# g0's rows turned by TensorE between idle matmuls, and the norm weights of the last row multiplied ahead of its norm

## The chip, the cores and the metric

The kernel runs on one core of one Trainium2 chip. A core has five engines that work side by side: TensorE (PE in the profile, its weight loads PEld), VectorE (DVE), ScalarE (ACT), GpSimd (POOL) and SyncE (SP). Each takes its own instructions in order; they wait for each other through semaphores. SyncE issues most transfers, ScalarE and GpSimd issue some; all of them run on the same 16 DMA engines. The metric is the time of one execution on the device, in microseconds (us), lower is better; the time before is the median of 3 runs.

## What is computed

A trunk of two layers over two independent sequences, a prompt of 2048 tokens and a sample of 512, with 1024 channels, all in float32:

```python
def trunk(x, ...):
    x = attention_layer(x, attn_norm[0], ...)     # layer 0
    x = fourier_layer(x, fourier_norm[0], ...)    # layer 1
    return rmsnorm(x, final_norm)

def rmsnorm(x, g):
    inv = lax.rsqrt(jnp.mean(x * x, axis=-1, keepdims=True) + 1e-6)
    return x * inv * g

def attention_layer(x, g, w_in, w_out, sink, rel_bias):
    z = rmsnorm(x, g) @ w_in                      # q, k, v and a gate
    o = banded_gqa_with_sink(q, k, v, rel_bias, sink)
    return x + (o * jax.nn.silu(gate)) @ w_out

def fourier_layer(x, g, w_gate, w_out):
    h = rmsnorm(x, g)
    f = jnp.fft.fftn(h.reshape(b, s, 4, 256), axes=(1, 3), norm="ortho").real
    return x + (f * jax.nn.silu(h @ w_gate)) @ w_out
```

`attn_norm[0]` is called g0 in the kernel, `final_norm` gf. The change touches how g0 reaches the chip's memory and how the last 128 rows of the result get their final norm.

## The kernel before

Tokens are worked on in tiles of 128 rows (the partitions of the on-chip memory). The attention phase takes five chunks of 512 tokens; chunk 0 is the sample. The Fourier phase follows and writes the outputs, a few tiles of 128 rows at a time.

Every float32 product is made of three: an operand is split into a coarse part (hi, a cast on ScalarE) and the rest (lo, a difference on VectorE or GpSimd), and `matmul3` (L92 to L95) adds hi*hi, hi*lo and lo*hi in one accumulator. So an operand takes two steps on two engines before its three matmuls can run, and all these matmuls stand under line 95 in the profile. A tile framework with its own scheduler places the instructions on each engine and sets the semaphores; `after(a, b)` only asks that a be issued behind b.

**The start.** At L61 to L63 the kernel makes small constants and asks, from ScalarE's queue, for g0 as a tile `g0s` of 128 partitions and 8 columns: partition p holds g0[k*128 + p] in column k. Twelve matmuls of zeros (`WARM`, L239 to L242) keep TensorE at work until the first operands are there; their zeros come from a VectorE memset. Meanwhile the first projection weight (k, 512 KB) comes in two halves, one from SyncE's queue and one from ScalarE's (`half`, L249 to L255), and is split into `wk`. `make_h` (L202) loads the transposed input in eight slices `xk` of 128 channels and 512 tokens, from SyncE's queue, and makes of each the scaled operand `h`: hi = xk*g0s on ScalarE (L220), lo = xk*g0s - hi on VectorE (L221). The norm's factor per token is applied later, to the products, so that nothing waits for it. `between` runs hooks behind a slice: behind slice 0 the split of the second half of `wk`, behind slice 3 the load and split of the second k weight (`load_w` with n = 9).

`kv_proj` (L302) then multiplies the eight h by the k weights into two accumulators (`spt`), and later by the v weights (`vp`); behind them come the q and gate products (`qp`, `gp`). The rows of the position bias are made by a small matmul (`bias_rows`, L262), copied out by VectorE, stored to device memory and read back as tiles `b`, which the scores of the attention use first.

**The end.** `Outs.products` (L1432 on) makes the last output rows: seven rounds of twelve matmuls, each added by VectorE to the residual rows `xa` and `xb` (`add`). For the very last tile (`last=True`) the sum of squares of `xb` is taken in two halves on ScalarE into two columns of `ss`: the second half early, the first half behind the last sum. VectorE adds the two, `inv_rms` (L86) makes mean plus epsilon on VectorE and the power -1/2 on GpSimd, and two VectorE products of three operands, x * inv * gf, one for each half, feed two stores, from SyncE's and ScalarE's queues:

```python
DVE.tensor_tensor(ss[:, 0:1], ss[:, 0:1], ss[:, 1:2], ALU.add)
inv = inv_rms(ss, 1, "invl")
for half in range(2):
    hs = q[half]
    DVE.scalar_tensor_tensor(xb[:, hs], xb[:, hs], inv[:, 0:1], gfb[:, hs], ALU.mult, ALU.mult)
    (SP, ACT)[half].dma_start(out_rows(self.us[1][1])[:, hs], xb[:, hs])
```

`gfb` holds gf in every partition; it is loaded long before.

Of the kernel before, what the change touches and what calls it, by code (L numbers as in the profile page):

```python
# [19 lines left out]
P = 128  # L20
D = 1024
# [3 lines left out]
KD = D // P  # L25
NH = 16
HD = 64
EPS = 1e-6
WARM = 12
BIG = 1.0e30  # L30
LINE = 512
LATE = (8, 9)
# [5 lines left out]
def f32(ap):  # L38
    return ap.bitcast(F32)
# [3 lines left out]
def encoder(  # L43
    ctx, tc, x, xT, w_in, w_out, rel_bias, sink, g0, onehot, w_gate, w_fout, g1, gf, chan, tabs, mirror, y_prompt, y_sample
):
    nc = tc.nc
    PE, ACT, DVE, POOL, SP = nc.tensor, nc.scalar, nc.vector, nc.gpsimd, nc.sync

    cpool = ctx.enter_context(tc.tile_pool(name="cpool", bufs=1))
    main = ctx.enter_context(tc.tile_pool(name="main", bufs=1))  # L50
# [12 lines left out]
    ACT.dma_start(g0s, g0.rearrange("(k p) -> p k", p=P))  # L63
# [13 lines left out]
    def bank(name):  # L77
        return banks[-1].tile([P, 512], F32, tag="bank", name=name)
# [7 lines left out]
    def inv_rms(ss, n, name, place=lambda ins: None):  # L86
        inv = main.tile([P, 8], F32, tag="inv", bufs=2, name=name)
        place(DVE.tensor_scalar(inv[:, :n], ss[:, :n], 1.0 / D, EPS, ALU.mult, ALU.add))
        POOL.tensor_tensor(inv[:, :n], inv[:, :n], mhalf[:, :n], ALU.pow)  # L89
        return inv  # L90
# [12 lines left out]
        last_fetch[0] = load  # L103
        return w32

    def load_w(c, n, name, lo_engine=None, late=None, w32=None):

        w = wp.tile([P, 2, D], F32R, align_bytes=LINE, tag="w", bufs=4, name=f"w{name}")
        if c == 1 and n in AGAIN:
            w32 = xtile([P, D], F32, f"w32{name}")  # L110
            SP.dma_start(w32, w_in[n])
            ACT.copy(w[:, 0], w32)
            DVE.tensor_tensor(w[:, 1], w32, f32(w[:, 0]), ALU.subtract)
            POOL.dma_start(f32(wsd[n]), f32(w))
            return w[:, 0], w[:, 1]
        if c:
            SP.dma_start(f32(w), f32(wsd[n]))
            return w[:, 0], w[:, 1]
        if w32 is None:
            w32 = fetch_w(n, name, late)  # L120
        ACT.copy(w[:, 0], w32)
        if lo_engine is None:

            for i in range(4):
                cs = slice(i * 256, i * 256 + 256)
                POOL.tensor_tensor(w[:, 1, cs], w32[:, cs], f32(w[:, 0, cs]), ALU.subtract)
        else:
            lo_engine.tensor_tensor(w[:, 1], w32, f32(w[:, 0]), ALU.subtract)
        if late or n not in LATE + AGAIN:
            (SP if lo_engine else POOL).dma_start(f32(wsd[n]), f32(w))  # L130
        return w[:, 0], w[:, 1]
# [17 lines left out]
    def attention_phase():  # L149

        with ExitStack() as es:
# [50 lines left out]
            def make_h(c, invb, between={}):  # L202
# [4 lines left out]
                for k in range(KD):  # L207
# [13 lines left out]
                    lo = DVE.scalar_tensor_tensor(h[:, 1, :], xk[:, :CH], gk, f32(h[:, 0, :]), ALU.mult, ALU.subtract)  # L221
                    after(hi, last_u[0])
                    after(lo, last_u[1])
                    hs.append((h[:, 0], h[:, 1]))
                    if k in between:
                        between[k]()
# [8 lines left out]
                return hs, halo  # L235


            idle = ap.tile([P, 512], BF16, tag="s", bufs=2, name="idle")
            DVE.memset(idle, 0.0)  # L239
            ps = bank("idle")  # L240
            for i in range(WARM):
                PE.matmul(ps, idle[:, :P], idle, start=True, stop=True)  # L242

            last_u = [None, None]

            wk = wp.tile([P, 2, D], F32R, align_bytes=LINE, tag="w", bufs=4, name="wk0_0")
            wk32 = stage[0]("w32k0_0")

            def half(i):  # L249
                cs = slice(i * 512, i * 512 + 512)  # L250
                (SP, ACT)[i].dma_start(wk32[:, cs], w_in[8, :, cs])
                return lambda: (
                    tc.keep_in_program_order(ACT.copy(wk[:, 0, cs], wk32[:, cs])),
                    DVE.tensor_tensor(wk[:, 1, cs], wk32[:, cs], f32(wk[:, 0, cs]), ALU.subtract),
                )  # L255

            halves = [half(i) for i in range(2)]
            halves[0]()
            early = [(wk[:, 0], wk[:, 1])]
            hs, halo = make_h(0, None, {0: halves[1], 3: lambda: early.append(load_w(0, 9, "k0_1", DVE))})  # L260

            def bias_rows():  # L262

# [656 lines left out]
    def fourier_phase(tail):  # L920
        with ExitStack() as es:
# [457 lines left out]
            class Outs:  # L1379
# [52 lines left out]
                def products(self, hooks, last=False):  # L1432
# [3 lines left out]
                    Z = psum2.tile([P, 512], F32, tag="acc", name=f"Zo{self.n}")  # L1436

                    def add(t, half, ps):
                        DVE.tensor_tensor(t[:, q[half]], t[:, q[half]], ps, ALU.add)

                    prod(W, A[0, 0], wo[0:4], four, True)
                    add(xa, 0, W)
# [31 lines left out]
                    ACT.activation(junk[:, :512], xb[:, q[0]], AF.Square, accum_out=ss[:, 0:1])  # L1474
                    DVE.tensor_tensor(ss[:, 0:1], ss[:, 0:1], ss[:, 1:2], ALU.add)
                    inv = inv_rms(ss, 1, "invl")
                    for half in range(2):
                        hs = q[half]
                        DVE.scalar_tensor_tensor(xb[:, hs], xb[:, hs], inv[:, 0:1], gfb[:, hs], ALU.mult, ALU.mult)
                        (SP, ACT)[half].dma_start(out_rows(self.us[1][1])[:, hs], xb[:, hs])  # L1480

            ft = {w: [] for w in ("T1", "T2", "T3", "N4")}
# [299 lines left out]
```

## Time and profile before

| what | value |
|---|---|
| median of 3 runs | 1589.11 us (1588.07 to 1589.41) |
| the profiled execution's own time | 1588.22 us |
| its span, first to last instruction | 1586.5 us |
| granted TensorE clock, mean | 0.999 |
| VectorE, ScalarE, GpSimd busy | 1153.0, 874.6, 445.6 us |
| data moved by DMA | 373.88 MB, mean 236 GB/s |

In the profile a line of a timeline reads: start, duration, engine and line of the kernel, operation, output and inputs with shapes, count, and in square brackets the idle time of that engine before it with what ended it. An engine name with a q (ACTq) is its queue, where it issues a transfer. A row of a view by stretches gives for a window of time the busy time of each engine with its count of instructions, then the granted clock, the busy share of the 16 DMA engines and the rate in GB/s. A row of DMA issues ends with the KB of one and the time from issue to landing.

### The profile page before, as it was taken

To read this page: it belongs to the slowest core of one execution; us is meant where nothing else is said; L and a number is where in the kernel's file an instruction comes from. 1 tells how busy PE (TensorE), PEld (TensorE's weight loads), DVE (VectorE), ACT (ScalarE), POOL (GpSimd) and SP (SyncE) were. 2 spreads that over 40 slices of the span, in tenths; PEclk is the share of its full clock that TensorE was granted. 3 is DMA by queue.
4 is the path that set the end of the run, shared out by engine and by line. 5 is a ranking of instruction groups with operands and counts; after the bars stand their busy time and mean duration, and the time that the engine had idled before them with its cause. 6 is when DMAs were issued, how large, how long until landed. Compare 5 with 4: busy or idle time off the path is not lost. (4 is left out here: it accounts for less than half of the span.)

```text
span 1586.5 us, 27419 instructions
## 1 busy us (share of the span) xinstructions
PE 1573.1 (99%) x9743; PEld 1321.4 (83%) x9743; DVE 1153.0 (73%) x2785; ACT 874.6 (55%) x2089; POOL 445.6 (28%) x613
## 2 busy tenths in 40 slices
PE   9999999999999999999999999999999999999998
PEld 7878888888888888988888888888888888888886
DVE  6788655887548786378764577669878878889796
ACT  6688534776246784167752476646555554343342
POOL 2466642421404314024222242223112111111010
PEclk9999999999999999999999999999999999999999
DMA  7588695565856567655649566665557469448752
GB/s 294 189 332 288 226 362 211 209 248 204 294 208 222 204 237 272 222 206 220 258 161 331 209 215 232 237 258 200 199 205 260 175 228 410 173 168 320 259 204 80
DMA packets 100580, 373.88 MB, mean 236 GB/s; under 512 B 12140, under 2 KB 22380, under 8 KB 83037
## 3 DMA queue, kind: packets, MB, share of 16 engines
q1 hardware_dynamic: 81708, 297.91, 52.4%
q0 software_dynamic: 16400, 70.04, 11.6%
q10 hardware_dynamic: 2336, 4.20, 0.7%
q8 instruction: 77, 1.26, 0.3%
q14 instruction: 59, 0.48, 0.1%
HBM read 280.84 MB, written 91.26 MB: 235 GB/s over the span
## 5 line engine op out<-in xcount | busy, mean ns | idle before, releaser
L489 DVE CUSTOM_DVE_ANT_0 S<-spt,b 128x385 f32<-128x385 f32 (+1 forms) x320 | 156.2, 527 | 114.5 <-PE spt L470 71.4
L95 PE MATMUL gp<-h,wg 128*128 128x512 f32 x960 | 237.6, 395 | 0.0
L95 PE MATMUL qp<-h,wq 128*128 128x512 f32 x960 | 237.3, 396 | 0.1
L95 PEld LDWEIGHTS qp<-h,wq 128*128 128x128 f32 x960 | 174.9, 188 | 37.3 <-DVE v L370 0.7
L95 PEld LDWEIGHTS gp<-h,wg 128*128 128x128 f32 x960 | 174.9, 188 | 37.1 <-issue 1.0
L497 ACT ACTIVATE S<-S 128x385 f32<-128x385 f32 (+1 forms) x320 | 188.8, 596 | 19.1 <-DVE S L489 18.6
L537 ACT CAST pts<-pt 128x384 fp32r<-128x384 f32 (+1 forms) x240 | 100.8, 461 | 176.6 <-PE pt L529 168.9
L538 DVE TENSOR_TENSOR pts<-pt,pts 128x384 fp32r<-128x384 f32 (+1 forms) x240 | 114.5, 523 | 18.9 <-ACT pts L537 18.8
L579 POOL TENSOR_TENSOR uT<-o,uT 128x256 fp32r<-128x256 f32 x75 | 55.4, 739 | 237.9 <-ACT uT L578 237.8
L95 PE MATMUL spt<-wo,uT 128*128 128x512 f32 x480 | 120.4, 391 | 0.0
L95 PE MATMUL op<-wo,uT 128*128 128x512 f32 x480 | 118.9, 391 | 0.0
L470 PE MATMUL spt<-kwin,qab 64*128 64x384 f32 (+1 forms) x960 | 118.6, 352 | 0.0
L555 PEld LDWEIGHTS av<-pts,v 128*128 128x128 f32 x576 | 101.3, 188 | 19.1 <-DVE pts L538 0.4
L555 PE MATMUL av<-pts,v 128*128 128x512 f32 (+1 forms) x576 | 115.9, 341 | 0.0
L95 PE MATMUL fo<-wo,tTu 128*128 128x512 f32 x480 | 115.3, 392 | 0.0
L95 PEld LDWEIGHTS op<-wo,uT 128*128 128x128 f32 x480 | 89.3, 188 | 18.6
L95 PEld LDWEIGHTS spt<-wo,uT 128*128 128x128 f32 x480 | 89.1, 188 | 18.4
L509 DVE TENSOR_SCALAR S<-S 128x384 f32<-128x384 f32 (+1 forms) x192 | 98.0, 511 | 6.8
L95 PEld LDWEIGHTS fo<-wo,tTu 128*128 128x128 f32 x480 | 88.3, 188 | 17.0
L470 PEld LDWEIGHTS spt<-kwin,qab 64*128 64x128 f32 x960 | 74.7, 186 | 28.4 <-issue 27.5
L575 POOL TENSOR_TENSOR o<-o,s 128x256 f32<-128x256 f32 x75 | 55.3, 737 | 132.0 <-DVE o L573 131.7
L529 PEld LDWEIGHTS pt<-ident,S 64*128 64x128 f32 x1344 | 79.0, 138 | 4.2 <-issue 1.9
(319 smaller groups left out, 3184.2 us busy)
## 6 DMA issues: line engine op xcount, KB each, us to landing
wo<-wsd SPq DMA_DIRECT2D x32, 1024.0 KB, 4.9
wq<-wsd SPq DMA_DIRECT2D x31, 1024.0 KB, 7.3
wg<-wsd SPq DMA_DIRECT2D x31, 1024.0 KB, 5.7
x<-x1d SPq DMA_DIRECT2D x40, 512.0 KB, 3.6
b<-b21d SPq DMA_DIRECT2D x40, 512.0 KB, 6.4
b<-rowd SPq DMA_DIRECT2D x40, 384.0 KB, 4.2
xs<-in_x_dram SPq DMA_DIRECT2D x23, 512.0 KB, 7.2
s2d<-gt POOLq DMA_DIRECT2D x40, 256.0 KB, 5.3
```

The lines of the kernel that those rows point to most:

```text
L95: pe(PE.matmul(out, a[i], b[j], start=start and i + j == 0, stop=stop and i == 1, skip_group_check=more))
L470: pe(PE.matmul(banks[j][:, 2 + k0 * P : 2 + k1 * P], res["q"][rows, qp, b * P : (b + 1) * P], kwin[g][rows, kp, b * P + k0 * P : b * P + k ...
L489: seq(DVE, DVE.tensor_tensor_reduce(out=s[:, e0:e1], in0=ps[:, 1 + e0 : 1 + e1], in1=st["bias"][:, j, 386 - e1 : 386 - e0][:, ::-1], scale ...
L497: last_exp[0] = seq(ACT, ACT.activation(s[:, e0:e1], s[:, e0:e1], AF.Exp, bias=s[:, 386:387], scale=-1.0, accum_out=s[:, 387:388]))
L509: seq(DVE, DVE.tensor_scalar(s[:, ks], s[:, ks], den, None, ALU.mult))
L529: pe(PE.transpose(ps[h][:, kb, j, :], ss[j][rows, 1 + kb * P : 1 + (kb + 1) * P], ident[rows, rows]))
L537: seq(ACT, ACT.copy(hi, ps[:, k0:k1]))
L538: seq(DVE, DVE.tensor_tensor(lo, ps[:, k0:k1], f32(hi), ALU.subtract))
L555: pe(PE.matmul(to, v, pt, start=n == part == 0, stop=part == 1 and n in (1, len(todo) - 1), skip_group_check=n > 1,))
L575: eng.tensor_tensor(o, o, s, ALU.mult)
L579: low = eng.tensor_tensor(lo, o, f32(hi), ALU.subtract)
```

## The change

Two places are edited, each with what it needs around it.

At the start, the request for g0 moves from the constants to just ahead of the first weight halves, still as the first transfer of ScalarE's queue, and asks for 8 rows of 128 elements (`g0r`) instead of 128 x 8 single ones. TensorE transposes the rows into an accumulator bank, and VectorE copies that to `g0s`. The idle matmuls are now 5 ahead of the transpose and 5 behind it, and take a constant of ones that exists anyway instead of a tile of zeros. Two order hints tie the split of the second k weight behind the operand of slice 3.

```diff
-WARM = 12
+WARM = 5
+MORE_WARM = 5
...
     g0s = cpool.tile([P, KD], F32, name="g0s")
-    ACT.dma_start(g0s, g0.rearrange("(k p) -> p k", p=P))
...
-    def load_w(c, n, name, lo_engine=None, late=None, w32=None):
+    def load_w(c, n, name, lo_engine=None, late=None, w32=None, behind=(None, None)):
...
-        ACT.copy(w[:, 0], w32)
+        hi = ACT.copy(w[:, 0], w32)
+        if lo_engine is DVE and n == 9:
+            after(hi, behind[0])
...
-            lo_engine.tensor_tensor(w[:, 1], w32, f32(w[:, 0]), ALU.subtract)
+            lo = lo_engine.tensor_tensor(w[:, 1], w32, f32(w[:, 0]), ALU.subtract)
+            if n == 9:
+                after(lo, behind[1])
...
                     after(lo, last_u[1])
+                    last_h[:] = hi, lo
...
-            idle = ap.tile([P, 512], BF16, tag="s", bufs=2, name="idle")
-            DVE.memset(idle, 0.0)
+            idle = nc.const_aps.tensor(1.0, [P, 512], BF16)
             ps = bank("idle")
             for i in range(WARM):
-                PE.matmul(ps, idle[:, :P], idle, start=True, stop=True)
+                warm = PE.matmul(ps, idle[:, :P], idle, start=True, stop=True)
...
+            g0r = ap.tile([KD, P], F32, tag="tmp", bufs=2, name="g0r")
+            ACT.dma_start(g0r, g0.rearrange("(k p) -> k p", p=P))
             halves = [half(i) for i in range(2)]
             halves[0]()
             early = [(wk[:, 0], wk[:, 1])]
-            hs, halo = make_h(0, None, {0: halves[1], 3: lambda: early.append(load_w(0, 9, "k0_1", DVE))})
+            gp = bank("g0t")[:, :KD]
+            turned = PE.transpose(gp, g0r, ident[:KD, :KD])
+            after(turned, warm)
+            DVE.tensor_copy(g0s, gp)
+            for i in range(MORE_WARM):
+                after(PE.matmul(ps, idle[:, :P], idle, start=True, stop=True), turned)
+            hs, halo = make_h(0, None, {0: halves[1], 3: lambda: early.append(load_w(0, 9, "k0_1", DVE, behind=last_h))})
```

At the end, for the last tile only, `xb` is multiplied by gf before the norm's factor is known. The early half of the sum of squares becomes half of the mean plus epsilon at once; when the other half is there, one VectorE instruction makes the mean. The second half of `xb` is multiplied by gf ahead of that instruction, the first half behind it, while GpSimd takes the power; then each half is multiplied by the factor alone.

```diff
                     def add(t, half, ps):
-                        DVE.tensor_tensor(t[:, q[half]], t[:, q[half]], ps, ALU.add)
+                        return DVE.tensor_tensor(t[:, q[half]], t[:, q[half]], ps, ALU.add)
...
-                    add(xb, 0, W)
+                    whole = add(xb, 0, W)
...
                     ACT.activation(junk[:, :512], xb[:, q[0]], AF.Square, accum_out=ss[:, 0:1])
-                    DVE.tensor_tensor(ss[:, 0:1], ss[:, 0:1], ss[:, 1:2], ALU.add)
-                    inv = inv_rms(ss, 1, "invl")
+                    sums = DVE.tensor_scalar(ss[:, 1:2], ss[:, 1:2], 1.0 / D, EPS, ALU.mult, ALU.add)
+                    after(sums, whole)
+                    inv = main.tile([P, 8], F32, tag="inv", bufs=2, name="invl")
+                    after(DVE.tensor_tensor(xb[:, q[1]], xb[:, q[1]], gfb[:, q[1]], ALU.mult), sums)
+                    mean = DVE.scalar_tensor_tensor(inv[:, 0:1], ss[:, 0:1], 1.0 / D, ss[:, 1:2], ALU.mult, ALU.add)
+                    after(DVE.tensor_tensor(xb[:, q[0]], xb[:, q[0]], gfb[:, q[0]], ALU.mult), mean)
+                    POOL.tensor_tensor(inv[:, 0:1], inv[:, 0:1], mhalf[:, 0:1], ALU.pow)
                     for half in range(2):
                         hs = q[half]
-                        DVE.scalar_tensor_tensor(xb[:, hs], xb[:, hs], inv[:, 0:1], gfb[:, hs], ALU.mult, ALU.mult)
+                        DVE.tensor_scalar(xb[:, hs], xb[:, hs], inv[:, 0:1], None, ALU.mult)
                         (SP, ACT)[half].dma_start(out_rows(self.us[1][1])[:, hs], xb[:, hs])
```

More of the change, by code (lines that the diff above doesn't have):

```diff
@@ L235, in make_h @@
                 return hs, halo
-            idle = ap.tile([P, 512], BF16, tag="s", bufs=2, name="idle")
-            DVE.memset(idle, 0.0)
+            idle = nc.const_aps.tensor(1.0, [P, 512], BF16)
             ps = bank("idle")
             for i in range(WARM):
-                PE.matmul(ps, idle[:, :P], idle, start=True, stop=True)
+                warm = PE.matmul(ps, idle[:, :P], idle, start=True, stop=True)
             last_u = [None, None]
+            last_h = [None, None]
             wk = wp.tile([P, 2, D], F32R, align_bytes=LINE, tag="w", bufs=4, name="wk0_0")
```

## The prediction, made before the changed kernel ran

> **What bounds the kernel now.** I read the page's engine shares first, then the waits of TensorE over the whole span, then the timeline of both ends, since the change touches only those.
>
> ```profile
> span 1586.5 us, 27419 instructions
> PE 1573.1 (99%) x9743; PEld 1321.4 (83%) x9743; DVE 1153.0 (73%) x2785; ACT 874.6 (55%) x2089; POOL 445.6 (28%) x613
> ```
> ```profile
> PE Ap L95 <- ACT gp L1310: 1.5, 1, 1.5
> ```
>
> TensorE is busy 1573.1 of 1586.5 us. Of the 13.4 us left, 1.8 lie in the first 7 us and some 7.5 behind the last matmul, as the rows below show; its longest wait is 1.5 us, far from both. In between, the stream of matmuls sets the pace, so what is won ahead of the first useful matmul moves everything behind it, and what is won behind the last one moves the end.
>
> **The head.** These are the rows of the timeline up to the first useful matmuls.
>
> ```profile
> 0.72 0.47 ACTq L63 DMA_DIRECT2D g0s<-in_g_dram  x1
> 0.73 0.39 SPq L251 DMA_DIRECT2D w32k<-in_w_in_dram  x1
> 0.85 0.27 DVE L239 MEMSET idle<- 128x256 uint32 x1 [0.85 <-PEq L1768]
> 1.18 5.30 PE L242 MATMUL idle<-idle 128*128 128x512 bf16 x12 [1.18 <-DVE idle L239]
> 1.85 1.28 ACT L253 ACT_TABLE_LOAD   x1 [1.85 <-issue]
> 4.01 0.62 ACT L253 CAST wk<-w32k 128x512 fp32r<-128x512 f32 x1 [0.88 <-DMA w32k<-in_w_in_dram]
> 4.66 0.69 DVE L254 TENSOR_TENSOR wk<-w32k,wk 128x512 fp32r<-128x512 f32 x1 [3.21 <-ACT wk L253]
> 6.28 0.72 ACT L220 ACTIVATE h<-xk,g0s 128x512 fp32r<-128x512 f32 x1 [1.66 <-DMA xk<-in_xT_dram]
> 7.04 0.75 DVE L221 SCALAR_TENSOR_TENSOR h<-xk,g0s,h 128x512 fp32r<-128x512 f32 x1 [1.69 <-ACT h L220]
> 7.06 11.55 PE L95 MATMUL spt<-h,wk 128*128 128x512 f32 x48 [0.57 <-ACT h L220]
> 7.84 10.34 PEld L95 LDWEIGHTS spt<-h,wk 128*128 128x128 f32 x46 [0.49 <-DVE h L221]
> 37.27 5.60 PE L95 MATMUL gp<-h,wg 128*128 128x512 f32 x24
> ```
>
> ScalarE makes h_0 at 6.28, after 1.66 us of waiting for the first slice of xT. The first useful matmul starts at 7.06, and from 7.84 the stream no longer breaks. One such matmul takes 5.60/24 = 0.23 us. Why xT is late is seen in the DMA view of four stretches (us; last columns: share of the 16 engines, GB/s), in the packets of the stretch 3 to 4, and in the issues:
>
> ```profile
> 2.00:3.00 1.00, 1.00 (x4) 0.44 (x3) 0.00 (x0) 1.00 (x1) 0.00 (x0) 1.00 0.82 209
> 3.00:4.00 1.00, 1.00 (x4) 0.32 (x3) 0.00 (x0) 0.13 (x1) 0.00 (x0) 1.00 0.49 34
> 4.00:5.00 1.00, 1.00 (x4) 0.30 (x3) 0.34 (x1) 0.62 (x1) 0.00 (x0) 1.00 0.81 247
> 5.00:6.00 1.00, 1.00 (x4) 0.30 (x2) 0.35 (x1) 0.00 (x0) 0.00 (x0) 1.00 1.06 408
> ```
> ```profile
> q10 hardware_dynamic: 699, 0.00, 38.0%
> ```
> ```profile
> g0s<-in_g_dram ACTq DMA_DIRECT2D x1, 4.0 KB, 4.5
> w32k<-in_w_in_dram SPq DMA_DIRECT2D x1, 256.0 KB, 3.3
> out_dram<-x SPq DMA_DIRECT2D x1, 256.0 KB, 2.0
> rb<-in_rel_bias_dram SPq DMA_DIRECT2D x1, 2.0 KB, 6.2
> ```
>
> The old request for g0 asks for 1024 single elements. 699 packets of ScalarE's queue (q10) fill the stretch 3 to 4, and the data rate falls from 209 to 34 GB/s; once they are gone it is 408. Against 408 the three stretches from 2 to 5 moved 490 KB instead of 1224, so the jam costs up to (1224-490)/408 = 1.8 us of transfer time.
>
> **The change at the head.** The load of g0 becomes 8 rows; the jam goes. In its place stands a chain: rows land, TensorE turns them, VectorE copies them to g0s, and h_0 waits for the copy. In the built program VectorE's copy stands behind the first split of wk, so both chains matter.
>
> The first half of w32k lands 3.3 us after its issue now; an undisturbed transfer of its size at the end of the kernel takes 2.0. That bounds its landing between 2.7 and 4.0. The table load ends at 3.13 anyhow; I take 3.3 for the cast, nearer to the undisturbed row. Then 0.62 for the cast, 0.69 for the split and two hand-overs of 0.03: 4.65. No row copies 8 columns out of PSUM. Its bounds are nothing and 0.69 (the split of 512 columns); I take 0.2, since a VectorE instruction on 16 columns takes 0.17:
>
> ```profile
> 16.09 0.17 DVE L278 TENSOR_SCALAR sk<-sk 128x16 f32<-128x16 f32 x1
> 25.83 0.60 PE L198 MATMUL spt<-ident,inv 128*128 128x128 f32 x4
> ```
>
> h_0 starts at 4.9, 1.4 us before the old 6.28. The slice of xT does not hold it: it shares the engines with the two halves of w32k, and if the first piece of 256 KB lands at 2.7 to 3.3 and two more follow at 408 GB/s (0.64 us each), the third is there at 4.0 to 4.6.
>
> TensorE: the idle matmuls need no memset now, so they start at about 0.9, where the memset did, and 5 of them at 5.30/12 = 0.44 end at 3.1. The rows of g0 land between 2.0 us (undisturbed) and 4.5 us (the old request) after 0.72; with 4 KB and nothing ahead I take 2.3, which is 3.0. The turn costs 0.15 to 0.3 (the row of four 128-column ones: 0.60), five more idle matmuls 2.2: from 3.1 TensorE is free at 5.6, just when h_0's first half is done (4.9+0.72). VectorE's half follows at 6.4 instead of 7.84, so 1.42 earlier. The built program no longer places the other bank's first matmul ahead of that wait, which leaves five matmuls of h_0 behind it instead of four: +0.23. This part gives **-1.2 us**.
>
> **The clock.** Idle matmuls run at 0.44 us, useful ones at 0.23, with the same 512 columns: TensorE is slow at first and turns fast between 5.85 and some 8 us. Useful matmuls that now start at 6.4 may still be slow; each us of that costs half a us, so between 0 and 0.8. I take 0.3. The Trainium skill (TensorE: Matmul & The Clock Gate, Part 1) states that the array starts at half clock and is released after a window of about 3.4 us of sustained work, a window that runs free of the kernel's start. By that the release would fall between 0.9+3.4 = 4.3 and 7.7 us, an estimate, and the cost between 0 and 0.65 from run to run; the trace agrees in so far as the first useful matmuls are fast.
>
> **Moves without a price.** The hook that ties the split of the second wk to h_3 leaves the order as it was. Past 18 us the scheduler moved the bias row's copy, the first bias load and a few casts. The load goes behind two weight loads, and ScalarE makes three casts of kwin ahead of v instead of two:
>
> ```profile
> 23.71 0.38 SPq L440 DMA_DIRECT2D b<-rowd  x1
> 31.70 5.31 PEld L95 LDWEIGHTS qp<-h,wq 128*128 128x128 f32 x24 [0.21 <-DVE v L370]
> 43.52 0.41 DVE L489 CUSTOM_DVE_ANT_0 S<-spt,b 128x257 f32<-128x257 f32 x1
> ```
>
> The bias is first used at 43.52, 20 us behind its issue; a delay of 2 to 3 us is covered by qp's and gp's matmuls. The further cast of 512 columns (0.62 in the row at 4.01) is hidden while ScalarE reaches v no later than v's matmuls end; the stream behind v waits only 0.21 today. Without that cover it costs up to 0.6; if the wait goes, -0.2. I take 0.
>
> **The tail.** From the last sum on:
>
> ```profile
> 1579.06 0.69 DVE L1439 TENSOR_TENSOR x<-x,Vo 128x512 f32<-128x512 f32 x1
> 1580.59 0.16 DVE L1475 TENSOR_TENSOR ssl<-ssl 128x1 f32<-128x1 f32 x1 [0.85 <-ACT jkl L1474]
> 1580.78 0.15 DVE L88 TENSOR_SCALAR invl<-ssl 128x1 f32<-128x1 f32 x1
> 1581.08 0.55 POOL L89 TENSOR_TENSOR invl<-invl,mhalf 128x1 f32<-128x1 f32 x1 [4.66 <-DVE invl L88]
> 1581.66 1.42 DVE L1479 SCALAR_TENSOR_TENSOR x<-x,invl,gfb 128x512 f32<-128x512 f32 x2 [0.73 <-POOL invl L89]
> 1582.44 0.33 SPq L1480 DMA_DIRECT2D out_dram<-x  x1
> 1583.11 0.34 ACTq L1480 DMA_DIRECT2D out_dram<-x  x1
> ```
>
> One small VectorE step goes (0.19): GpSimd's power could start at 1580.9. The multiply of the second half by gfb fits into the 0.85 us in which VectorE waits. The multiply of the first half does not: it starts beside the power. Elsewhere the trace has that pair:
>
> ```profile
> 1356.94 0.68 DVE L1311 TENSOR_TENSOR gp<-e,gp 128x512 fp32r<-128x512 f32 x1
> 1357.17 0.86 POOL L89 TENSOR_TENSOR invf<-invf,mhalf 128x1 f32<-128x1 f32 x1 [11.46 <-DVE invf L88]
> ```
>
> A power takes 0.55 alone, but 0.86 when a VectorE product of two SBUF tiles started 0.23 before it. In the new tail the product runs from 1580.65 to 1581.33, so I take 0.86: the power ends at 1581.76, against 1581.63 now. The Trainium skill (GPSIMD Engine Reference, 1. Specifications) states that GpSimd's SBUF interfaces are shared with VectorE and contend with instructions of two SBUF inputs; it speaks against this edit, and that row agrees. By the rule the tail gives the -0.2 below, by the lone 0.55 it would give -0.6. The two last products lose their second tile. Bounds: 0.42 (the cast of 512 columns from SBUF to SBUF) and 0.75 (as now); I take 0.45, nearest to rows with one SBUF input:
>
> ```profile
> L309 DVE CAST kwin<-kwin x12: 415/416/807, 271.3 to 805.3; 128x512 fp32r<-128x512 f32 x12
> L509 DVE TENSOR_SCALAR S<-S x192: 354/423/991, 255.8 to 1021.9; 128x384 f32<-128x384 f32 x168, 128x256 f32<-128x256 f32 x24
> ```
>
> The first store is issued at 1581.78+0.45+0.03 = 1582.26 (now 1582.44), the second at about 1582.7 (now 1583.11). Both share the engines, and 512 KB take 1.3 us at 408 GB/s, so the end follows the first issue: **-0.2**. Bounds are -0.6 (power at 0.55) and +0.1 (products at 0.75).
>
> **The sum.** -1.2+0.3-0.2 = -1.1 us. Against the profiled execution's own 1588.22 (span 1586.5, the rest launch) that gives 1587.1; its median of three runs is 1589.11, which gives 1588.0. I forecast halfway, **1587.6**.
>
> **The rivals.**
> 1. The clock is released late. The idle work is now cut in two by the wait for g0. If the count begins anew at 3.4 and takes as long as now, from 1.18 to between 5.85 and 7.06, it comes at 8.1 to 9.3: useful matmuls lose up to (9.3-6.4)/2 = 1.45, and the head gives +0.25. With the tail, nothing is left: 1588.7, halfway between the two times of before. For it: all twelve idle matmuls ran slow. Against: the gap is a fraction of a us.
> 2. Slower: g0's rows land late. Everything on TensorE then hangs on the turn and the five idle matmuls behind it. Today the six matmuls of h_0 end at 7.84 plus four of 0.23, or 8.8. Landing 6.2 us after issue, as the 2 KB of rb did, is 6.9; with 0.3, 2.2 and six of 0.23 they end at 10.8: +2.0, with the tail +1.8, or 1590.5. It decides from a landing at 5.1, where these steps make up for the tail as well. Against: rb stood behind a 512 KB load, these rows behind nothing, and even the old request came at 5.2.
> 3. Every unknown falls well: fast clock at once, split done at 4.5, power undisturbed, qp free: -1.5-0.6-0.2 = -2.3, or 1586.4.
>
> **How the numbers follow.** Forecast 0.69, rival 1 0.12, rival 2 0.07, rival 3 0.12. What a measurement of this kernel can tell is about 0.2%, 3.2 us, far over the sum. Runs of one kernel lie up to 1.3 us apart (1588.07 to 1589.41), so only a part of rival 3 (0.08) can pass it on the fast side and a part of rival 2 (0.04) on the slow one; 0.88 stays within. The range, 1585.8 to 1589.8, runs from rival 3 less half that spread to rival 1 and most of it.
>
> **What would show it.** Right: no fall of the data rate between 2 and 5 us, h_0 at 4.6 to 5.2, first useful matmul at 5.3 to 6.0, the last power near 0.86 us, the last products under 0.5. Wrong: h_0 waiting for g0s with VectorE long idle (rival 2), useful matmuls at 0.43 us beyond 8 us (rival 1), or a new wait of TensorE between 10 and 45 us.

## The result and the profile after

The changed kernel takes 1591.82 us in the median of 22 runs (1590.04 to 1594.73), the kernel before 1588.35 us in 22 runs beside it (1587.55 to 1591.24): a ratio of 1.0020 with an interval of [1.0014, 1.0027], some 3 us slower. The forecast was 1587.6, at most 1589.8.

The page and TensorE's waits of the changed kernel (engine, line and tile that waits, what it waits for; us in total, times, longest):

```profile
span 1588.5 us, 27420 instructions
```
```profile
PE spt L95 <- ACT h L224: 1.6, 1, 1.6
PE Ap L95 <- ACT gp L1323: 1.5, 1, 1.5
...
PE qp L95 <- DVE v L383: 0.9, 1, 0.9
```

The profiled execution took 1590.25 us with a span 2.0 longer than before. The wait of 1.5 was there before. Two are new: one ahead of the first h, and one at qp, where there had been 0.21.

The head, in the timeline of the changed kernel (start, duration, instruction, idle time before it and what ended it):

```profile
0.72 0.59 ACTq L263 DMA_DIRECT2D g0r<-in_g_dram  x1
...
2.99 0.27 PE L268 MATMUL g0t<-ident,g0r 8*128 8x8 f32 x1
3.19 1.74 PE L272 MATMUL idle<-const-bfloat16-1.0 128*128 128x512 bf16 x5
...
5.04 0.16 DVE L270 COPY g0s<-g0t 128x8 f32<-128x8 f32 x1
5.74 0.72 ACT L224 ACTIVATE h<-xk,g0s 128x512 fp32r<-128x512 f32 x1 [1.34 <-DMA xk<-in_xT_dram]
...
6.51 0.50 PE L95 MATMUL spt<-h,wk 128*128 128x512 f32 x1 [1.58 <-ACT h L224]
...
7.30 0.95 PE L95 MATMUL spt<-h,wk 128*128 128x512 f32 x2 [0.28 <-DVE h L225]
```

The rows of g0 are turned at 2.99, and the first useful matmul starts at 6.51 instead of 7.06. But the five idle matmuls end at 4.93 and TensorE then stands for 1.58 us, since h_0 waits for its slice of xT. The windows of the changed kernel (last columns: granted clock, DMA share, GB/s) show what became of the jam, and what came behind the gap:

```profile
3.00:4.00 1.00, 1.00 (x4) 0.44 (x4) 0.00 (x0) 0.25 (x2) 0.00 (x0) 1.00 0.88 301
...
7.00:8.00 1.00, 0.72 (x3) 0.61 (x3) 1.00 (x3) 1.00 (x2) 0.00 (x0) 0.81 1.05 426
8.00:9.00 1.00, 1.00 (x4) 0.75 (x3) 1.00 (x2) 0.87 (x3) 0.00 (x0) 0.50 1.00 391
...
11.00:12.00 1.00, 1.00 (x6) 0.79 (x5) 1.00 (x3) 1.00 (x3) 0.00 (x0) 0.98 1.02 418
```

The stretch from 3 to 4 moves 301 GB/s where it moved 34: the jam is gone. The clock however is halved from 7.6 to 11.0, which costs 3.4/2 = 1.7 us, more than the 0.55 that the head had won in this profile. And there is a second loss behind 18 us. This is the stretch in the timeline of the kernel before,

```profile
18.54 1.03 PE L271 MATMUL bp<-oh,rb 33*16 33x512 f32 x2
...
19.50 6.49 PE L95 MATMUL vp<-wv,h 128*128 128x256 f32 x52
19.60 0.68 DVE L273 COPY brow<-bp 16x512 f32<-16x512 f32 x1 [3.34 <-PE bp L271]
...
26.46 0.59 ACT L199 COPY invb<-spt 128x512 f32<-128x512 f32 x1 [3.95 <-PE spt L198]
...
28.05 0.20 ACT L452 COPY b<-sk 128x4 f32<-128x4 f32 x1
```

and in that of the changed kernel:

```profile
19.79 1.03 PE L284 MATMUL bp<-oh,rb 33*16 33x512 f32 x2
...
20.75 7.79 PE L95 MATMUL vp<-wv,h 128*128 128x256 f32 x60
...
21.44 0.67 DVE L286 COPY brow<-bp 16x512 f32<-16x512 f32 x1
...
25.82 0.89 SPq L453 DMA_DIRECT2D b<-rowd  x2
...
28.38 0.60 PE L202 MATMUL spt<-ident,inv 128*128 128x128 f32 x4
...
29.53 0.20 ACT L465 COPY b<-sk 128x4 f32<-128x4 f32 x1 [1.34 <-DMA b<-rowd]
29.63 0.58 ACT L203 COPY invb<-spt 128x512 f32<-128x512 f32 x1
...
33.68 0.87 DVE L383 SCALAR_TENSOR_TENSOR v<-vp,vsc,v 128x256 fp32r<-128x256 f32 x2
...
34.22 0.96 PE L95 MATMUL qp<-h,wq 128*128 128x512 f32 x3 [0.94 <-DVE v L383]
```

Two instructions have changed places in their engines' order. VectorE's copy of the bias row (`brow`) came right behind bp's matmul; now it stands behind the norm's mean and two steps that use the power. One of the v accumulators takes bp's bank next, so TensorE waits for that copy (0.28 us here). And ScalarE's copy of the sink into `b` came behind `invb`, the norm's factors for the k products; now it stands ahead of them and waits 1.34 us for b's load. Behind `invb` come the scaling of k, its casts and v, and qp waits for v. The load itself is later too: its first part is issued at 25.82 instead of 23.71. In the kernel before that part took 4.3 us to land, at about 28.0, just ahead of the copy at 28.05: there was no slack.

Where the 2.0 us of the profiled execution came from (us; positions from the timelines):

| position | before | after | step |
|---|---|---|---|
| first useful matmul | 7.06 | 6.51 | -0.55 |
| bias row's matmul (bp) | 18.54 | 19.79 | +1.80: half clock 1.7 |
| qp | 31.70 | 34.22 | +1.27: vp 0.28, qp 0.94 instead of 0.21; 0.26 not placed |
| first scores | 42.80 | 45.34 | +0.02 |
| last sum of the tail | 1579.06 | 1580.98 | -0.62 |
| end of the span | 1586.5 | 1588.5 | +0.1 |

The step of -0.62 lies within the scatter: in the profiles here the scores and the last sum lie 1535.0 to 1537.4 us apart, whatever the start.

The tail of the changed kernel:

```profile
1580.98 0.69 DVE L1452 TENSOR_TENSOR x<-x,Vo 128x512 f32<-128x512 f32 x1
...
1582.82 0.86 POOL L1494 TENSOR_TENSOR invl<-invl,mhalf 128x1 f32<-128x1 f32 x1 [4.48 <-DVE invl L1492]
1583.72 0.88 DVE L1497 TENSOR_SCALAR x<-x,invl 128x512 f32<-128x512 f32 x2 [0.44 <-POOL invl L1494]
1584.24 0.34 ACTq L1498 DMA_DIRECT2D out_dram<-x  x1
1584.63 0.33 SPq L1498 DMA_DIRECT2D out_dram<-x  x1
```

The power takes 0.86 and ends 2.70 behind the start of the last sum; the two stores are issued 3.26 and 3.65 behind it, where it was 3.38 and 4.05. The last transfer lands 5.91 behind it instead of 6.06, but the span ends 7.50 behind it instead of 7.39. The two stores have also changed places: ScalarE's queue now issues first and SyncE's last. In every profile with the new tail the span ends 1.58 to 1.59 us behind the last landing, in the three with the old one (before, e1, e10) 1.34; that eats the 0.15 won at the landing. Whether the exchange of the stores makes this difference was not tried. The tail is worth nothing that shows.

### The profile page after: what moved, and what is told of

The parts are those of the page before. It is cut to its first block, busy times and chain, and to the rows that moved or that the text cites. A ratio compares the mean times of both kernels' runs of the same rounds, so it can differ in the third digit from the quotient of the medians.

```text
span 1588.5 us, 27420 instructions
## 1 busy us (share of the span) xinstructions
PE 1573.3 (99%) x9742; PEld 1322.5 (83%) x9742; DVE 1152.1 (73%) x2787; ACT 875.0 (55%) x2089; POOL 447.0 (28%) x613
```

## The experiments

All runs below were compared with the kernel before on the same chip. Where nothing else is said, the diff is against the changed kernel.

| run | first useful | vp waits for the bank | qp waits for v | clock halved | scores | median us | ratio to before |
|---|---|---|---|---|---|---|---|
| changed | 6.51 | 0.28 | 0.94 | 7.6-11.0 | 45.34 | 1591.82 | 1.0020 [1.0014, 1.0027] |
| e1 | 6.06 | 1.41 | 0.34 | 21.8-25.2 | 45.78 | 1590.24 | 1.0016 [1.0007, 1.0025] |
| e2 | 6.46 | none | 0.65 | no | 42.90 | 1588.55 | 1.0002 [0.9993, 1.0011] |
| e3 | 5.99 | 3.01 | 0.34 | 24.2-27.6 | 47.02 | 1592.92 | 1.0031 [1.0019, 1.0043] |
| e4 | 6.09 | none | 2.36 | 35.0-38.4 | 46.18 | 1589.68 | 1.0009 [1.0000, 1.0018] |
| e5 | 7.48 | none | none | 8.1-11.6 | 44.94 | 1588.83 | 1.0001 [0.9992, 1.0010] |
| e6 | 6.01 | 1.39 | none | no | 43.61 | 1589.90 | 1.0011 [1.0002, 1.0020] |
| e7 | 5.96 | none | 2.89 | no | 44.83 | 1591.10 | 1.0019 [1.0010, 1.0028] |
| e8 | 5.98 | none | 3.37 | 34.6-38.0 | 46.91 | 1591.51 | 1.0026 [1.0016, 1.0036] |
| e9 | 6.03 | none | none | no | 41.83 | 1587.10 | 0.9993 [0.9984, 1.0002] |
| e10 | 6.09 | none | none | no | 41.99 | 1587.43 | 0.9995 [0.9986, 1.0004] |
| e11 | 5.89 | 2.22 | 0.34 | 22.7-26.1 | 46.11 | 1591.49 (one run) | |
| e12 | 6.04 | none | none | no | 41.97 | 1587.32 | 0.9995 [0.9986, 1.0004] |
| e13 | 5.95 | 2.21 | 0.33 | 22.8-26.2 | 46.24 | 1590.99 | 1.0017 [1.0008, 1.0026] |
| e14 | 5.94 | none | 0.34 | slow until about 10 | 43.86 | 1588.17 | 0.9997 [0.9988, 1.0006] |

The middle columns are those of one profiled execution each, the last two of all runs; kernels with the same start differ by chance in the first and in the clock.

**e1, the head alone**: the changed kernel with the old tail.

```diff
-                    sums = DVE.tensor_scalar(ss[:, 1:2], ss[:, 1:2], 1.0 / D, EPS, ALU.mult, ALU.add)
...
+                    DVE.tensor_tensor(ss[:, 0:1], ss[:, 0:1], ss[:, 1:2], ALU.add)
+                    inv = inv_rms(ss, 1, "invl")
```

> The changed start with the old end. Theory: the whole loss comes from the start, half of it from TensorE's clock (halved again for 3.4 us after the idle matmuls ran out ahead of h_0) and half from the order that the scheduler made behind it. Then this is as slow as the changed kernel: 2.5 to 4 us over before, and the first qp matmul starts 1.5 to 3.5 us later than 31.70. Rival (the start won its 1.2 us and the end lost more): 0.5 to 1.5 us faster than before.

The loss is there without the new tail: 1590.24, 2.0 over before where 2.5 to 4 was expected, with a vp wait of 1.41 that was not in the list of the first profile, and a half clock at another place. So one profile of the changed kernel does not show all that its start costs.

**e2, the tail alone**: the kernel before with the new tail (the second diff of the change).

> The old start with the changed end; up to the last sum the order of every engine is that of before. Theory: the end is worth next to nothing, since GpSimd's power takes 0.86 us beside the product with gf where it took 0.55: between -0.4 and +0.2 us against before. Rival (the end is the loss): 2 to 4 us slower.

1588.55 beside 1588.24: no difference that shows. The loss comes with the new start. This profile shows one thing more. With the old start and the old order, its first useful matmul ran at 6.46, 0.60 earlier than in the profile of before, and bp at 17.97, 0.57 earlier. Yet qp starts at 31.77, where it was 31.70:

```profile
28.16 0.20 ACT L452 COPY b<-sk 128x4 f32<-128x4 f32 x1 [0.73 <-DMA b<-rowd]
...
31.77 4.40 PE L95 MATMUL qp<-h,wq 128*128 128x512 f32 x18 [0.65 <-DVE v L370]
```

The sink's copy waits for b's load, v comes behind it on ScalarE, and qp waits 0.65. So even in the old order what TensorE wins at the head stops at b's load.

**e3, the gap filled**: twelve idle matmuls behind the turn.

```diff
-MORE_WARM = 5
+MORE_WARM = 12
```

> The changed kernel with 12 idle matmuls behind the transpose instead of 5. Theory of the clock: with fast idle matmuls (0.23 us) they end at 6.3, right ahead of h_0; TensorE has no gap, the granted clock stays at 1.0 between 7 and 11 us, and the stream reaches the bias rows' matmul at about 18.2 instead of 19.79; if the clock is still low when they run (0.43 us each) they end at 8.3 and hold the first useful matmul up instead. Median 1 to 2 us below the changed kernel, and less spread than its 1590.0 to 1594.7. Rival (the clock does not hang on the gap): no gain, or the 7 further idle matmuls cost 1 to 2 us.

The rival: no gain. The gap ahead of h_0 is gone, the first useful matmul is at 5.99 and the clock full, and yet it is the slowest of all. The clock behind the gap at h_0 is thus not the whole cause: the earlier TensorE arrives at vp, the longer it waits there (3.01), since the norm's mean, which stands ahead of the bias row's copy, depends on the token tiles and not on TensorE.

**e4, the old order**: what had moved behind 18 us is put back by hints.

```diff
+        if c == 0 and n == 1:
+            after(hi, kcasts[1])
...
-                    lambda: inv_rms(ss, nt, f"inv{c}", lambda ins: seq(DVE, ins) if c > 1 else None)
+                    lambda: inv_rms(ss, nt, f"inv{c}", lambda ins: seq(DVE, ins) if c > 1 else after(ins, None if c else row[0]))
...
-                    ACT.copy(invb[:, i0 * P : (i0 + m) * P], ps[:, : m * P])
+                    spread_out[0] = ACT.copy(invb[:, i0 * P : (i0 + m) * P], ps[:, : m * P])
...
-                DVE.tensor_copy(brow, bp[:NH])
+                row[0] = DVE.tensor_copy(brow, bp[:NH])
...
+                                if len(kcasts) > 2:
+                                    after(kc, vcasts[1 if len(kcasts) < 5 else 3])
...
+                    elif c == 0:
+                        after(ends, spread_out[0])
```

(`ends` is the sink's copy, `kcasts` and `vcasts` collect the casts of kwin and v; the four transposes that spread the norm also stand ahead of the fifth slice's v matmuls.)

> The changed kernel with hints that put the scheduler's order between 19 and 40 us nearly back: the bias row's copy ahead of the norm's factor, the factor's transposes ahead of the fifth slice's matmuls, ScalarE's fill of the bias tile and the cast of wq_1 behind invb, two casts of kwin ahead of v. Theory of the order: qp starts without the 0.94 us of waiting, about 1.3 us earlier against the bias rows' matmul than in the changed kernel (14.4 us behind it there, 13.2 in before), and the median falls by 1 to 2 us. Rival (only the clock matters): qp keeps its distance or TensorE's wait moves elsewhere, median within 0.5 us of the changed kernel.

vp no longer waits, but the sink's copy, again between invb and the casts as in the kernel before, waits 3.46 us for b's load and holds v:

```profile
29.41 0.20 ACT L474 COPY b<-sk 128x4 f32<-128x4 f32 x1 [3.46 <-DMA b<-rowd]
```

qp waits 2.36, so the theory of the order failed there, though the median fell by some 2 us. In its old place the copy now waits because the load is late. The bias row is stored at 19.97, earlier than the 20.60 of before, but the store takes 5.6 us to land instead of 3.1, and b's load is issued at 25.54 instead of 23.71. Two weight loads have moved ahead of b's load; the DMA engines move 385 GB/s from 23 to 24 us, where before the rate had fallen to 43 from 22 to 23. That these two loads delay the store is likely; no run took them away.

**e5, the sink's copy behind the casts too**, against e4:

```diff
-                        after(ends, spread_out[0])
+                        after(ends, kcasts[-1])
```

> The changed kernel with five moves undone behind 18 us: the bias row's copy again ahead of the norm's mean on VectorE, the spread of the norm ahead of the fifth slice's v matmuls, two kwin casts ahead of v, the second q weight's cast behind those two, and (new against the run before) ScalarE's sink copy into b behind the last kwin cast, so that no wait for b's load stands ahead of v. Theory (the head's gain is lost in waits that the new order makes behind 18 us): vp waits 0, v is ready some 5.9 us behind a spread at 24.7, or 30.6, ahead of the end of vp's matmuls at about 31.1, so qp starts at 31.0 to 31.5 without a wait of 0.5 us or more, the scores at 42.1 to 42.6 (42.80 before), last matmul 0.3 to 0.7 earlier than before; time 1587.3 to 1588.4, that is 0 to 0.9 below the kernel before. Rival (the new start itself costs, by the clock or by the other placement of data, wherever the waits lie): 1589.7 or more, as in the run with the wait of b.

No wait of vp or qp is left, as the theory had it, and the time falls to 1588.83, level with before but 0.4 above the range expected. In its profile the slice of xT came late (h_0 at 6.70), and there is a half clock from 8.1 to 11.6 behind a gap of 2.3 us.

**e6, e5 with nine idle matmuls** (`MORE_WARM = 9`).

> The same order with nine idle matmuls behind the turn of g0 in place of five, so that TensorE has no gap of a us or more ahead of h_0. Theory: the nine end within 0.4 us of h_0's first half (5.99 to 6.5), the clock is full from about 4 us on and not halved between 7 and 12 us, first useful matmul 6.0 to 6.5, and since no wait behind 18 us takes the gain away, the time is that of the same order with five or up to 1 us less: 1586.9 to 1588.2, which would be the first kernel at or below the one before. Rival (with the earlier arrival TensorE waits again, as with twelve idle matmuls in the changed order): a new wait of 0.5 us or more between 18 and 35 us and 1588.5 or more.

The rival: vp waits 1.39 again. With this count the program had the split of the second v weight ahead of the bias row's copy on VectorE.

**e7, the bias row's copy alone put back.**

```diff
-                    lambda: inv_rms(ss, nt, f"inv{c}", lambda ins: seq(DVE, ins) if c > 1 else None)
+                    lambda: inv_rms(ss, nt, f"inv{c}", lambda ins: seq(DVE, ins) if c > 1 else after(ins, None if c else row[0]))
...
-                DVE.tensor_copy(brow, bp[:NH])
+                row[0] = DVE.tensor_copy(brow, bp[:NH])
```

> The changed kernel with one move undone: the bias row's copy ahead of the norm's mean on VectorE, all other moves kept. Theory: vp's wait for the bank (0.28 in the changed kernel's profile, 1.41 and 3.01 where the start came earlier) goes, but spread, casts and the wait for b's load stay, so qp still waits 0.9 us or more for v and starts at 33.3 to 34.2; time between the changed kernel and the run with the old order, 1590.0 to 1591.7. Rival (the bank alone is the cause): no wait of TensorE of 0.5 us or more behind 18 us, 1588.5 or less.

**e8, the bias row's product in an accumulator of its own.**

```diff
-                bp = bank("bp")
+                bp = spt[3]
```

> The changed kernel with the bias row's product in an accumulator that chunk 0 leaves unused until the scores, instead of the bank that a v product takes next; nothing else differs up to there but the place of one small memset. Theory: as with the copy put first, vp's wait for the bank goes and the late spread is what is left: qp waits 0.9 us or more for v, 1590.0 to 1591.7. Rival (the bank alone): no such wait, 1588.5 or less.

In both the wait only moves on, as the theory had it. The timeline of e7:

```profile
18.63 7.45 PE L95 MATMUL vp<-wv,h 128*128 128x256 f32 x60
...
25.92 0.60 PE L203 MATMUL spt<-ident,inv 128*128 128x128 f32 x4
...
29.02 0.20 ACT L466 COPY b<-sk 128x4 f32<-128x4 f32 x1 [3.29 <-DMA b<-rowd]
29.12 0.58 ACT L204 COPY invb<-spt 128x512 f32<-128x512 f32 x1
...
33.71 2.58 PE L95 MATMUL qp<-h,wq 128*128 128x512 f32 x10 [2.89 <-DVE v L384]
```

vp runs through, the norm is spread at 25.92, 2.5 us earlier than in the changed kernel; then ScalarE stands for 3.29 us at the sink's copy with invb behind it, and qp pays 2.89. In e8 it is 3.37. So the bank alone is not the cause.

**e9, e6 with the bias row's copy ahead of that split:**

```diff
             if n == 9:
                 after(lo, behind[1])
+            elif c == 0 and n == 11 and row[0] is not None:
+                after(lo, row[0])
```

> The same as the run with the old order and nine idle matmuls, and in addition the bias row's copy ahead of the split of the second v weight on VectorE, where it stood before the change. Theory (what is left over is the 1.4 us that vp waited for the bank): vp waits 0, qp starts at 31.0 to 31.4 without a wait of 0.5 us or more, the scores at 42.0 to 42.4 (42.80 before, 43.61 with the wait), the clock is not halved before the last matmul; time 1.0 to 1.5 us below the run with nine idle matmuls and the wait (1589.9), that is 1588.3 to 1588.9 and no slower than the kernel before within its interval; by the profile's own span 1585.4 to 1586.0. Rival (every us won on the way to qp comes back as a wait for the v or k operands, whose chain starts at the x tiles and not at TensorE): qp waits 0.5 us or more and starts at 31.7 or later, time 1589.5 or more.

The timeline of e9:

```profile
6.03 11.60 PE L95 MATMUL spt<-h,wk 128*128 128x512 f32 x48
...
18.52 6.01 PE L95 MATMUL vp<-wv,h 128*128 128x256 f32 x48
18.62 0.68 DVE L291 COPY brow<-bp 16x512 f32<-16x512 f32 x1 [3.25 <-PE bp L289]
...
30.72 5.51 PE L95 MATMUL qp<-h,wq 128*128 128x512 f32 x23
```

No wait at h_0, vp or qp; the scores start at 41.83, 0.97 earlier than before, and the span is 1584.8. The time is better than the 1588.3 to 1588.9 expected: 1587.10, beside 1588.67 for the kernel before.

**e10, e9 with the old tail** (the diff of e1).

> The kernel with the old order, nine idle matmuls and the copy ahead of the v split, but with the tail of before (sum, mean, power, two products of three operands). Theory (the new tail is worth nothing): last sum to the end of the span 7.4 us as before, the power 0.55 us, the time within 0.5 us of the same kernel with the new tail. Rival (the tail is worth the 0.2 to 0.6 that the prediction gave at its bounds): 0.2 to 0.6 us slower than with the new tail.

1587.43 against 1587.10 with the new tail, and 7.42 us from the last sum to the end of the span against 7.50: the new tail gives nothing that shows.

**e11, the changed kernel again, for a second profile.**

> The changed kernel itself once more, for a second profile: its profiled execution of 1590.25 was among the fastest of its 22 runs (median 1591.82). Theory: the runs nearer the median lose the rest in the same two places, a longer wait of vp or qp behind 18 us, or one more window of half clock of 3.4 us (worth 1.7) behind a gap of TensorE of 1 us or more; the last matmul's place less that of the scores stays within 1 us of the 1535.4 seen. Rival: the rest is lost elsewhere, in the later phases, and that difference is 1 us or more longer.

It took 1591.49, near the median. Its timeline:

```profile
18.51 1.33 PE L95 MATMUL vp<-wv,h 128*128 128x256 f32 x9
...
21.35 0.67 DVE L286 COPY brow<-bp 16x512 f32<-16x512 f32 x1
...
22.07 7.86 PE L95 MATMUL vp<-wv,h 128*128 128x256 f32 x51 [2.22 <-DVE brow L286]
```

The slice of xT came in time, the first useful matmul ran at 5.89 and vp was reached 2.2 us earlier than in the first profile. The bias row's copy however came at 21.35, where it had been 21.44. All that was won became a wait of 2.22, a half clock from 22.7 to 26.1 came on top (1.7 us), and the scores started at 46.11, later than in the first profile. The theory's places held.

**e12, e9 once more.**

> The kernel with the old order behind 18 us, nine idle matmuls and the new tail a second time, since its interval against the kernel before (0.9984 to 1.0002) just reached no change. Theory (the head's gain of about 1 us stays once nothing behind it waits): median 1586.7 to 1587.9, ratio to the kernel before 0.9990 to 0.9998, scores at 41.8 to 42.3 in the profile, vp and qp without a wait of 0.5 us. Rival (the first median was a lucky one): 1588.2 or more, ratio 0.9999 or more.

1587.32 beside 1588.07. Each of the intervals of e9 and e12 still reaches just past 1.

**e13, the sink's copy alone moved**, as in e5:

```diff
+                    elif c == 0:
+                        after(ends, kcasts[-1])
```

> The changed kernel with one instruction moved: ScalarE's copy of the sink into b, which waits for b's load, stands behind the last kwin cast instead of ahead of the norm's copy out (invb); all else is the changed kernel. Theory (two waits in one chain: vp's for the bank, then ScalarE's for b's load ahead of invb, kwin and v): the bank's wait of 0.3 to 2.3 us stays, the wait for b's load ahead of invb goes, qp's wait falls below 0.5 us; time between the kernel before and the changed one, 1589.0 to 1591.0. Rival (the late spread and the third cast hold v, b's load does not): qp waits 0.9 us or more and the time is the changed kernel's, 1591.0 to 1592.0.

**e14, e13 and e7 together**: two instructions moved, all else as in the changed kernel.

> The changed kernel with two instructions moved: the sink's copy as in the run beside it, and the bias row's copy ahead of the norm's mean. Theory (these two make the loss): vp waits 0, spread at about 25.9, invb right behind it at 26.5 instead of 29.12, v ready 4.6 us later at 31.1, so qp starts at 31.0 to 31.4 after 0.2 to 0.6 us of waiting, the scores at 42.0 to 42.6; time 1587.3 to 1588.9, level with the kernel before or up to 1 us below, more only where the clock is halved behind the gap ahead of h_0. Rival (late spread, casts and the load's place make it): qp waits 1 us or more, starts at 32 or later, time 1589.5 or more.

The timeline of e13,

```profile
22.16 7.86 PE L95 MATMUL vp<-wv,h 128*128 128x256 f32 x51 [2.21 <-DVE brow L287]
...
30.50 0.59 ACT L204 COPY invb<-spt 128x512 f32<-128x512 f32 x1 [0.82 <-PE spt L203]
...
35.10 1.21 PE L95 MATMUL qp<-h,wq 128*128 128x512 f32 x4 [0.33 <-DVE v L386]
```

and of e14:

```profile
20.22 7.46 PE L95 MATMUL vp<-wv,h 128*128 128x256 f32 x60
...
28.15 0.59 ACT L205 COPY invb<-spt 128x512 f32<-128x512 f32 x1 [0.82 <-PE spt L204]
...
32.75 3.47 PE L95 MATMUL qp<-h,wq 128*128 128x512 f32 x14 [0.34 <-DVE v L387]
```

The changed kernel, e7, e13 and e14 are a square. With both instructions in their new places the time is 1591.82; with the bias row's copy put back 1591.10; with the sink's copy behind the casts 1590.99; with both 1588.17. Either wait alone costs nearly all of it, because both hold the same chain (the norm's spread, invb, k, v) and the longer hides the other. In e14 invb follows its transposes at once and qp waits 0.34. Its qp and scores are later than expected, at 32.75 and 43.86, by a clock that was slow until about 10 us. So these two account for the loss.

But e14 does not restore the old order. The sink's copy stands behind the casts, further back than in the kernel before; there the late load of b costs nothing. With the copy in its old place, in e4, it costs a wait of 2.36 at qp. The late spread and the third cast ahead of v, both still there in e14, cost no more than the 0.34 in this profile.

## Why the prediction was wrong

The step that failed is "Moves without a price", taken as 0. It says that the bias "is first used at 43.52, 20 us behind its issue; a delay of 2 to 3 us is covered by qp's and gp's matmuls". The first user is not the scores but ScalarE's copy of the sink, at 28.05 in the kernel before, 4.3 us behind the issue and right behind the landing. In the profiles v follows it on ScalarE, and in the changed program invb as well; so the delay of 2.1 us had no cover. For the bias row's copy the step gave no price at all; it did not ask which matmul takes bp's bank next. The runs put about 3.6 us in place of that 0: 1588.17 with both dealt with (e14, 0.9997 of the kernel before) against 1591.82 (1.0020). The prediction named a new wait of TensorE between 10 and 45 us as what would prove it wrong, and that came.

The premise that "what is won ahead of the first useful matmul moves everything behind it" failed by the same chain. The wait of 0.21 at qp, which the prediction read, says that v was already the last to come. In e2 the old start came 0.60 earlier and qp did not move.

The other terms, by their own steps:

- **The jam**: right. 301 GB/s in place of 34 between 3 and 4 us, and the rows of g0 turned at 2.99 where 3.0 was worked out.
- **h_0 at 4.9 and TensorE free at 5.6**: half right. VectorE's copy of g0s came at 5.04; in e7, e9, e11, e13 and e14 the first useful matmul ran at 5.89 to 6.03, 1.0 to 1.2 ahead of the profile of before, near the -1.2 of the sum. Against the 6.46 that the old start also reached (e2), it is 0.4 to 0.6. The step "the slice of xT does not hold it" failed in the first profile (5.74) and in that of e5 (6.70). And the idle matmuls behind the turn took 1.74 in the first profile instead of 2.2; with the late slice that left the gap.
- **The clock, +0.3**: too small for five idle matmuls. It was 1.7 in the first profile and in that of e5, nearly as much in e14's, and nothing at the head in the other six with that start. With nine, four profiles (e6, e9, e10, e12) show no loss. The prediction saw only a late release of the clock (rival 1, at 8.1 to 9.3). The clock records begin at 3.7 to 5.7 us in all profiles of the new start but e14's, where they begin at 10.2; in the first profile and e5's the clock was full and was halved again behind the gap.
- **The tail, -0.2**: steps right, end wrong. The power ended 2.70 behind the last sum, as worked out, and the stores went out at 3.26 and 3.65 where 3.20 and 3.64 follow from the text. The last landing is 0.15 earlier, but the span ends later behind it (7.50 against 7.39 from the last sum). What sets the end behind the last landing, no run here shows.
- **The noise.** The prediction took 0.2% as what a measurement can tell. The interval of the result is 0.07% to either side, so the loss of 0.20% is clear.

The mechanism of the head was right as far as the first useful matmul. With the bias row's copy early, the sink's copy behind the casts and the gap filled (e9, e12), the medians lie 1.6 and 0.8 us under the kernel before, about the -1.1 of the sum. With intervals that touch 1, that it is faster is likely but not shown. Nor is it shown how much of it is the head's: no run has the old start with the sink's copy behind the casts.

## What to carry to other kernels

When a change lets the scheduler place instructions anew, go through every instruction that changed places on an in-order engine and ask two things: what does it wait for itself, and who stands behind it; the first user of a transfer may be a small copy long before the large one. Where the main stream already waits for another chain, here 0.21 us, what is won ahead of it stops there. An engine that comes earlier to a buffer that another chain frees does not win, it waits longer, and the gap can cost more than it lasted by the clock. Of two waits in one chain, undoing one shows little: try them alone and together.

## What the runs showed of the hardware

**The clock behind a gap.** Eight profiles (the changed kernel, e1, e3, e4, e5, e8, e11, e13) have one stretch of half clock of 3.4 us behind a gap of TensorE of 1.4 to 3.4 us, and it begins 0.1 to 1.6 us behind the end of that gap. Others with such a gap have none: e6 with 1.39 and e7 with 2.89, or the kernel before with 1.5 in mid-run. The windows of e7 and e8, behind a wait of 2.89 and of 3.37:

```profile
34.00:38.00 4.00, 4.00 (x19) 3.25 (x19) 3.50 (x9) 3.40 (x6) 2.52 (x4) 1.00 0.23 94
```
```profile
34.00:38.00 4.00, 3.81 (x10) 3.03 (x11) 3.53 (x9) 3.85 (x7) 2.04 (x3) 0.57 0.39 164
```

19 matmuls in the one, 10 in the other. In every trace the clock records change only at multiples of 3.41 us behind the first of them, so it matters how a gap lies in these stretches. In seven of the eight profiles TensorE stood for 1.86 us or more in one stretch, and the next ran at half clock. The wait of e7 was cut in two by a border at 32.07, 1.25 and 1.65, and the kernel before had at most 1.51 in a stretch: no half clock. e1 does not fit: it lost the clock behind 1.40, where e6 with 1.39 kept it. Why is open.

The Trainium skill (TensorE: Matmul & The Clock Gate, "Why this matters for your kernels") says to leave no gap over about 3 us; six of the eight gaps here were 2.4 us or shorter, down to 1.4, so the measurement is harsher. The Trainium skill (TensorE: Matmul & The Clock Gate, Part 1) also has a window of about 3.4 us that runs free of the kernel's start; the stretches of 3.41 us here agree, and their first border lies elsewhere from run to run.

**A granted clock of 1.00 that is not one.** The view by windows shows 1.00 where the records of the clock have not begun yet. In e14 they begin at 10.2, and until then the matmuls are slow; these are its windows:

```profile
6.00:8.00 2.00, 2.00 (x4) 1.31 (x5) 2.00 (x4) 2.00 (x4) 0.00 (x0) 1.00 1.02 391
8.00:10.00 2.00, 2.00 (x6) 1.52 (x6) 1.36 (x3) 1.42 (x3) 0.00 (x0) 1.00 1.04 402
```

10 matmuls of 512 columns ran in 4 us, where e9 ran 20 in the same stretch. At the start the count of matmuls tells more than the clock's column.

**GpSimd beside VectorE.** The power took 0.86 in the new tails (0.87 in e13), where a VectorE product of two SBUF tiles runs beside it, and 0.55 in the old ones (before, e1, e10), as the pair of rows in the prediction had it. The Trainium skill (GPSIMD Engine Reference, 1. Specifications) states that GpSimd shares its SBUF interfaces with VectorE and contends with VectorE instructions of two SBUF inputs. These runs agree, and 0.86 was the right price for the power.
